# The down projection of a SwiGLU block: from a plain blocked product to Strassen's seven products

## The chip, the cores and the metric

The kernel runs on one core of a Trainium2 chip. Its engines work side by side, each on its own queue of instructions in a fixed order: PE (TensorE) multiplies matrices into PSUM, DVE (VectorE), ACT (ScalarE) and POOL (GpSimd) work elementwise, and SP (SyncE) issues loads and stores, which 16 DMA engines carry out. The metric is the device time of one execution in microseconds (us), lower being better.

## What is computed

One layer of an audio encoder on 1024 frames of width 1024, all in float32. The change touches only the last matrix product, `w_down`; the lines around it:

```python
x = x + rms_norm(mix, post_mix_g[l])
h2 = rms_norm(x, pre_ffn_g[l])
f = (jax.nn.silu(h2 @ w_gate[l]) * (h2 @ w_up[l])) @ w_down[l]
x = x + rms_norm(f, post_ffn_g[l])
```

`w_gate` and `w_up` are 1024 x 2816, `w_down` is 2816 x 1024. Below, f is the hidden activation, the product of silu(gate) and up; it is stored transposed, 22 blocks of 128 hidden rows by 1024 frames.

## The kernel before

**Precision.** Each float32 operand is split into a high half `hi` (ACT, L78, a cast) and a low half `lo` (DVE, L79, operand minus `hi`). A product then takes three matmuls: hi with hi, hi with lo, lo with hi (L103 to L105, or L1032 to L1034 in gate and up). Every matmul here is 128 x 128 stationary by 128 x 512 moving.

**Gate and up** (class `Gemm`, about 640 to 1098 us) already use Strassen's scheme in Winograd's form: 22 small products, a gate and an up product for each of 11 pairs p of hidden blocks, each made of seven sub-products q of 12 matmuls. POOL makes sums of weight pieces (`wsum`, L997), ACT and DVE split them into `whi` and `wlo` (four buffers each), PE multiplies into the PSUM banks `px`, `pz`, `py`, and ACT and DVE combine the results into `c` tiles. The sub-products of neighbouring gemms are interleaved by the list `order`. `finish` (L1058 to L1066) multiplies each up tile by its gate tile on DVE (L1065), and POOL stores it to `fd` in DRAM (L1066); four tiles of 128 x 512 belong to a pair p: two hidden blocks by two halves of the frames.

**Down** (`down_block`, `down_mm`, from L1092). The two column halves `dh` of the output are done one after the other. For each, eight PSUM banks hold the eight row tiles of the output, and PE runs over all 22 hidden blocks k: 8 row tiles x 3 matmuls for one k, so 2 x 22 x 8 x 3 = 1056 matmuls. The blocks k are fed in groups of mostly four: SP loads f (two tiles for a k, L1110) and `w_down` (one, L1114) into eight `raw` buffers (`wraw`, `ld`, `Td`), f is split into `fb`, of which there are two (tag `T`), and the weight into `whi` and `wlo`. Between the column halves the eight banks are read out: DVE copies (L1169), ACT sums squares (L1171), POOL multiplies by the gain (L1172). The last group of the second half runs row tile by row tile, with norm and store (L1126, L1127) right behind each.

**Order.** A scheduler fixes the order on every engine when the program is built. Loads and splits of a group stand under `tc.high_priority()`, so they come as early in the queues as free buffers allow; on ACT and DVE they can stand ahead of work that was written earlier. PSUM has eight banks: four of tag `b` (`pB`), two of `a` (`pA`), `c0` and `c1` (`pS`).

Of the kernel before, what the change touches and what calls it, by code (L numbers as in the profile page):

```python
# [41 lines left out]
def tile_hymba_trunk(ctx, tc, x, w_in, vecs, w_l, w2, a2, g2, w_o, w_gate, w_up, w_down,  # L42
# [21 lines left out]
    def v1(col):  # L64
# [1031 lines left out]
    def bank(i):
        if i < 4:
            return pB.tile([128, H], F32, name="pd", tag="b")
        if i < 6:
            return pA.tile([128, H], F32, name="pd", tag="a")  # L1100
        return pS.tile([128, H], F32, name="pd", tag=f"c{i - 6}")

    def down_block(ks, dh):
        fb = tp.tile([128, 4, 2, 2, H], F32R, name="fb", tag="T")
        ws = []
        with tc.high_priority():
            for n, k in enumerate(ks):
                for h in range(2):
                    raw = raw_tile([128, H])
                    sy.dma_start(out=raw, in_=fd[k][:, h * H:(h + 1) * H])  # L1110
                    split(raw, fb[:, n, h, 0], fb[:, n, h, 1])
                    if h == 0:
                        raw = raw_tile([128, H])
                        sy.dma_start(out=raw, in_=w_down[k * 128:(k + 1) * 128, dh * H:(dh + 1) * H])  # L1114
                        ws.append(wsplit(raw, [128, H]))
        return fb, ws

    def down_mm(ps, fb, ws, n, k, i):
        f = fb[:, n, i // 4]
        ts = slice((i % 4) * 128, (i % 4 + 1) * 128)  # L1120
        mm3(ps, f[:, 0, ts], f[:, 1, ts], ws[n][0], ws[n][1], k == 0, k == NHID - 1)

    def close(i, xts, rs):
# [5 lines left out]
    acc1 = {}  # L1129
    for dh, sizes in ((0, (4, 4, 4, 4, 4, 2)), (1, (4, 4, 4, 4, 2, 4))):  # L1130
        pd = [None] * 8
        k0 = 0
        for bn, size in enumerate(sizes):
            ks = range(k0, k0 + size)
            k0 += size
            fb, ws = down_block(ks, dh)
            if dh == 0 or bn < len(sizes) - 1:
                for n, k in enumerate(ks):
                    for i in range(8):
                        if k == 0:  # L1140
                            pd[i] = bank(i)
                        down_mm(pd[i], fb, ws, n, k, i)
                continue
            prev = None
            for i in range(8):
                xts = []
                for q in range(2):
                    xt = wt("xt", XT[(2 * i + q) % len(XT)], [128, H])
                    sy.dma_start(out=xt, in_=x1d[i * 128:(i + 1) * 128, q * H:(q + 1) * H])
                    xts.append(xt)  # L1150
                for n, k in enumerate(ks):
                    down_mm(pd[i], fb, ws, n, k, i)
                junk = wt("junk", "Vtok", [128, H])
                sc.activation(junk, pd[i], AF.Square, accum_out=ssqs[i][:, 1:2])
                a = acc1[i] = wt("acc1", "am", [128, H])
                ve.tensor_tensor(out=a, in0=pd[i], in1=gain[1][:, H:D], op=ALU.mult)
                ss = sp.tile([128, 1], F32, name="ss1", tag="ss1")
                gp.tensor_tensor(out=ss, in0=ssqs[i][:, 0:1], in1=ssqs[i][:, 1:2], op=ALU.add)
                rs = rsqrt_rows(sp, ss, D, "fo", gp)
                if prev:  # L1160
                    close(*prev)
                prev = (i, xts, rs)
            close(*prev)
        if dh == 0:
            for i in range(8):
                ssq = sp.tile([128, 2], F32, name="ssf", tag=f"ssf{i}", bufs=1)
                ssqs.append(ssq)
                a = wt("acc0", ("e", "ez")[i // 4], [128, H])
                ve.tensor_copy(out=a, in_=pd[i])  # L1169
                junk = wt("junk", "Vtok", [128, H])  # L1170
                sc.activation(junk, pd[i], AF.Square, accum_out=ssq[:, 0:1])  # L1171
# [68 lines left out]
```

## Time and profile before

| | us |
|---|---|
| time, median of 3 runs (1356.93 to 1358.76) | 1358.42 |
| the profiled execution's own time | 1353.48 |
| span from its first to its last instruction | 1351.7 |
| PE busy / DVE busy / ACT busy / POOL busy | 1287.8 / 882.7 / 505.3 / 332.6 |
| down projection, first to last matmul | 1086.4 to 1343.7 |

The profile is one execution. A row of an engine gives start and duration; "idle before" or the bracket behind a row is the time the engine stood still ahead of it and what ended that. Matmuls overlap, so their start-to-start distance, not their duration, is what one costs.

### The profile page before, as it was taken

How to read it: one execution, taken by the hardware profiler on the slowest of the kernel's cores; microseconds unless marked ns; L12 is line 12 of the kernel's file. 1: busy time of each engine (PE TensorE's matmuls, PEld its weight loads, DVE VectorE, ACT ScalarE, POOL GpSimd, SP SyncE). 2: the span in 40 equal slices, each digit the busy share in tenths (PEclk: the TensorE clock that was granted, in tenths of full speed). 3: DMA queues.
4: the chain of work that ended last, by engine and by line, in shares of the span. 5: the costliest groups of instructions: out<-in, count | busy, mean ns of one | idle time of the engine just before them, and what ended most of it. 6: DMA issues, size and time to landing. Idle time of an engine off the chain costs nothing.

```text
span 1351.7 us, 21475 instructions
## 1 busy us (share of the span) xinstructions
PE 1287.8 (95%) x8184; PEld 1027.6 (76%) x8184; DVE 882.7 (65%) x1690; ACT 505.3 (37%) x939; POOL 332.6 (25%) x376
## 2 busy tenths in 40 slices
PE   7999899999989999999889999999999989998997
PEld 5878767777767777677668888888888868887886
DVE  5999899988898885554885555455545453335335
ACT  7237336334322223434443333333333343234231
POOL 1122315232323111042533333323323200003002
PEclk9999899899989999999999999999999999999999
DMA  6116334222221103542312222222222274433525
GB/s 235 32 47 210 102 110 131 71 89 87 73 86 56 64 6 111 183 163 94 125 55 92 80 86 78 94 77 88 71 79 86 86 241 134 148 130 124 166 94 202
DMA packets 70663, 144.84 MB, mean 107 GB/s; under 512 B 8352, under 2 KB 8736, under 8 KB 70560
## 3 DMA queue, kind: packets, MB, share of 16 engines
q1 hardware_dynamic: 61376, 118.30, 27.1%
q0 software_dynamic: 5728, 18.88, 3.7%
q10 hardware_dynamic: 3456, 6.29, 1.2%
q8 instruction: 64, 1.05, 0.3%
q14 instruction: 39, 0.32, 0.1%
HBM read 106.74 MB, written 36.70 MB: 106 GB/s over the span
## 4 chain that ended last, share of the span: by engine, by line
PE 45%; DVE 2%; DMA 2%; issue 1%; ACT 1%; POOL 0%; DVEq 0%; SPq 0%; ACTq 0%; POOLq 0%
PE px L1032 5%; PE px L1033 5%; PE px L1034 5%; PE pd L104 5%; PE pd L103 5%; PE pd L105 5%; PE pz L1032 3%; PE pz L1033 3%; PE pz L1034 3%; PE py L1034 1%; PE py L1033 1%; PE py L1032 1%; DMA wraw<-fd 1%; DVE fb L79 1%; DVE wlo L79 0%
## 5 line engine op out<-in xcount | busy, mean ns | idle before, releaser
L79 DVE TENSOR_TENSOR wlo<-wraw,whi 128x512 fp32r<-128x512 f32 x155 | 109.5, 707 | 153.8 <-ACT whi L78 151.7
L78 ACT CAST whi<-wraw 128x512 fp32r<-128x512 f32 x155 | 95.9, 620 | 225.0 <-PE pd L105 77.5
L103 PE MATMUL pd<-whi,fb 128*128 128x512 f32 x352 | 137.4, 392 | 8.2 <-ACT junk L1171 4.0
L104 PE MATMUL pd<-wlo,fb 128*128 128x512 f32 x352 | 137.7, 391 | 0.0
L105 PE MATMUL pd<-whi,fb 128*128 128x512 f32 x352 | 137.6, 391 | 0.0
L79 DVE TENSOR_TENSOR fb<-wraw,fb 128x512 fp32r<-128x512 f32 x88 | 61.3, 737 | 70.4 <-ACT fb L78 70.0
L78 ACT CAST whi<-wsum 128x512 fp32r<-128x512 f32 x88 | 54.5, 619 | 122.5 <-PE py L1033 36.1
L79 DVE TENSOR_TENSOR wlo<-wsum,whi 128x512 fp32r<-128x512 f32 x88 | 66.8, 759 | 45.5 <-ACT whi L78 44.5
L250 DVE SCALAR_TENSOR_TENSOR cfa<-cfu,vec,cfa 128x512 f32<-128x512 f32 x120 | 92.4, 798 | 0.8
L997 POOL TENSOR_TENSOR wsum<-wraw 128x512 f32<-128x512 f32 x44 | 59.6, 1354 | 114.3 <-DMA wraw<-in_w_gate 42.2
L103 PE MATMUL prkv<-hT,whi 128*128 128x512 f32 x192 | 82.7, 430 | 2.6 <-DVE lz L369 2.6
L103 PEld LDWEIGHTS pd<-whi,fb 128*128 128x128 f32 x352 | 66.4, 189 | 24.0 <-ACT junk L1171 4.9
L575 DVE TENSOR_TENSOR tm<-TT,Mg 128x2 f32<-128x2 f32 (+30 forms) x248 | 79.4, 320 | 5.9
L78 ACT CAST fb<-wraw 128x512 fp32r<-128x512 f32 x88 | 50.5, 619 | 77.0 <-PE pd L105 43.4
L105 PE MATMUL prkv<-hT,wlo 128*128 128x512 f32 x192 | 78.8, 410 | 0.0
L104 PE MATMUL prkv<-hT,whi 128*128 128x512 f32 x192 | 78.4, 408 | 0.0
L105 PEld LDWEIGHTS pd<-whi,fb 128*128 128x128 f32 x352 | 66.5, 189 | 14.1
L104 PEld LDWEIGHTS pd<-wlo,fb 128*128 128x128 f32 x352 | 66.5, 189 | 13.6
L1032 PE MATMUL px<-h2T,whi 128*128 128x512 f32 x176 | 70.1, 398 | 1.8 <-ACT c L1046 1.4
L1033 PE MATMUL px<-h2T,whi 128*128 128x512 f32 x176 | 69.5, 395 | 0.0
L1034 PE MATMUL px<-h2T,wlo 128*128 128x512 f32 x176 | 69.4, 394 | 0.0
L577 DVE TENSOR_REDUCE TT<-tm 128x1 f32<-128x2 f32 (+30 forms) x248 | 62.9, 253 | 5.8
(335 smaller groups left out, 3155.5 us busy)
## 6 DMA issues: line engine op xcount, KB each, us to landing
wraw<-fd SPq DMA_DIRECT2D x88, 256.0 KB, 3.6
wraw<-in_w_in SPq DMA_DIRECT2D x44, 256.0 KB, 2.9
wraw<-in_w_gate SPq DMA_DIRECT2D x44, 256.0 KB, 2.8
wraw<-in_w_up SPq DMA_DIRECT2D x44, 256.0 KB, 2.8
fd<-c POOLq DMA_DIRECT2D x44, 256.0 KB, 2.3
wraw<-in_w_down SPq DMA_DIRECT2D x44, 256.0 KB, 3.3
xt<-in_x SPq DMA_DIRECT2D x16, 512.0 KB, 4.6
mix<-m POOLq DMA_DIRECT2D x24, 256.0 KB, 2.4
```

The costliest lines, as they stand in the source:

```text
L78: sc.copy(hi, raw)
L79: ve.tensor_tensor(out=lo, in0=raw, in1=hi.bitcast(F32), op=ALU.subtract)
L103: te.matmul(ps, lhsT=lhi, rhs=rhi, start=start, stop=False)
L104: te.matmul(ps, lhsT=lhi, rhs=rlo, start=False, stop=False)
L105: te.matmul(ps, lhsT=llo, rhs=rhi, start=False, stop=stop)
L250: ve.scalar_tensor_tensor(out=acc, in0=u[:, q:q + H], scalar=v1(V_CFW + i * 31 + q), in1=acc, op0=ALU.mult, op1=ALU.add)
L575: ve.tensor_tensor(out=tm[:, 0:ni, 0:t + 1], in0=TT[:, 0:ni, 0:t + 1], in1=Mg[:, t, 0:t + 1].unsqueeze(1).to_broadcast([128, ni, t + 1]), ...
L577: ve.tensor_reduce(out=TT[:, 0:ni, t:t + 1], in_=tm[:, 0:ni, 0:t + 1], axis=AX.X, op=ALU.add)
L997: gp.tensor_tensor(out=t, in0=x, in1=y, op=op)
L1032: te.matmul(ps, lhsT=hi[:, k, :], rhs=rhi, start=first and k == 0, stop=False, skip_group_check=True)
L1033: te.matmul(ps, lhsT=hi[:, k, :], rhs=rlo, start=False, stop=False, skip_group_check=True)
L1034: te.matmul(ps, lhsT=lo[:, k, :], rhs=rhi, start=False, stop=k == 3, skip_group_check=True)
```

## The change

The down projection is done by the same seven-product scheme. The output is seen as 2 x 2 blocks (two halves of the frames by two column halves), f and `w_down` as 2 x 2 blocks for each pair p of hidden blocks (first or second block of the pair). A step is one product q of one pair p: its f operand (128 x 512) and its weight operand (128 x 512) are each split in two, and it takes 4 row tiles x 3 = 12 matmuls. There are 7 x 11 = 77 steps, so 924 matmuls, in the order of `PQ`: all pairs of product 1, then of 5, 6, 3, 7, 2, 4. The products 1, 6, 7, 4 accumulate in the four banks `X` (tag `b`), 5, 3, 2 in `Z` (tags `a`, `c0`, `c1`); behind each product `after` reads its banks out while the next product uses the other four.

The f operands that are sums (products 5, 6, 7, 3) are made under gate and up: `finish` makes four sums `fs` on DVE for each pair, and POOL stores them by one DMA of 1 MB to `fsd`; of the four f tiles three are still stored. The weight operands that are sums are made on DVE in the down projection (`d_operand`), 44 subtractions in all. Both operands of a step go through `ob` (tag `T`, two buffers of four steps each); the weights no longer go through `whi` and `wlo`. The groups are 18 of four steps, one of one, one of four, and the last runs row tile by row tile.

The core of the diff:

```diff
-    t2r = mp.tile([128, 4, H], F32, name="t2r")
+    t2r = wt("t2r", "t2r", [128, 4, H])
...
-                gp.dma_start(out=fd[2 * self.p + b][:, h * H:(h + 1) * H], in_=dst)
+                f = self.done
+                f[b, h] = dst
+                q = {(0, 0): 1, (1, 0): 2, (1, 1): 4}.get((b, h))
+                if q:
+                    gp.dma_start(out=fd[q, self.p], in_=dst)
+                if len(f) == 4:
+                    fs = wt("fs", "t2r", [128, 4, H])
+                    for n, (x, y, op) in enumerate(((f[0, 1], f[1, 1], ALU.add), (fs[:, 0], f[0, 0], ALU.subtract),
+                                                    (f[0, 0], f[0, 1], ALU.subtract), (f[1, 0], fs[:, 1], ALU.subtract))):
+                        ve.tensor_tensor(out=fs[:, n], in0=x, in1=y, op=op)
+                    gp.dma_start(out=fsd[self.p], in_=fs)
...
+    PQ = [1, 5, 6, 3, 7, 2, 4]
+    steps = [(q, p) for q in PQ for p in range(NP)]
...
+        if q == 5:
+            if p % 2 == 0:
+                t = wt("tres", ("AR", "ZA")[p // 2 % 2], [128, 2, H])
+                tres[p], tres[p + 1] = t[:, 0], t[:, 1]
+            x, y = d_raw(p, 0, 1), d_raw(p, 0, 0)
+            ve.tensor_tensor(out=tres[p], in0=x, in1=y, op=ALU.subtract)
+            return tres[p]
+        if q == 6:
+            x = d_raw(p, 1, 1)
+            ve.tensor_tensor(out=tres[p], in0=x, in1=tres[p], op=ALU.subtract)
+            return tres[p]
+        x = d_raw(p, 0 if q == 7 else 1, 0)
+        a, b = (tres[p], x) if q == 7 else (x, tres[p])
+        ve.tensor_tensor(out=x, in0=a, in1=b, op=ALU.subtract)
+        return x
...
+    def down_block(block):
+        ob = tp.tile([128, 4, 2, 2, H], F32R, name="ob", tag="T")
         with tc.high_priority():
+            for n, (q, p) in enumerate(block):
+                split(f_raw(q, p), ob[:, n, 0, 0], ob[:, n, 0, 1])
+                split(d_operand(q, p), ob[:, n, 1, 0], ob[:, n, 1, 1])
+        return ob
+
+    def down_mm(q, p, ob, n, t):
+        f, w = ob[:, n, 0], ob[:, n, 1]
+        ts = slice(t * 128, (t + 1) * 128)
+        ps = (Z if q in (5, 3, 2) else X)[t]
+        st, en = q in (1, 5, 2) and p == 0, p == NP - 1
+        te.matmul(ps, lhsT=f[:, 0, ts], rhs=w[:, 0], start=st, stop=False, skip_group_check=True)
+        te.matmul(ps, lhsT=f[:, 0, ts], rhs=w[:, 1], start=False, stop=False, skip_group_check=True)
+        te.matmul(ps, lhsT=f[:, 1, ts], rhs=w[:, 0], start=False, stop=en, skip_group_check=True)
...
+    KEPT = {1: ["e"] * 4, 5: ["ez"] * 4, 6: ["am"] * 3 + ["hs"]}
...
+    def after(q, t):
+        if q in KEPT:
+            k = kept[q, t] = wt("kept", KEPT[q][t], [128, H])
+            sc.copy(k, (Z if q == 5 else X)[t])
+        elif q == 3:
+            c = kept[6, t]
+            ve.tensor_tensor(out=c, in0=Z[t], in1=c, op=ALU.add)
+            square(t, 1, c)
+            scaled(c, 1, gp)
...
+        else:
+            square(4 + t, 0, X[t])
+            a = wt("c21", "bv", [128, H])
+            ve.tensor_tensor(out=a, in0=X[t], in1=gain[1][:, 0:H], op=ALU.mult)
+            row_out(4 + t, (a, kept[5, t]), *row_scale(4 + t))
+
+    sizes = [4] * 18 + [1, 4]
```

Three places show how the built order moves. First DVE in gate and up, behind the last tile of a pair (`c` with two numbers is the multiplication by the gate tile; `wlo` is a low half of a gate or up weight). Before:

```order
L1065 TENSOR_TENSOR c_9781<-c_9781,c_9629 128x512
L79 TENSOR_TENSOR wlo<-wraw,whi 128x512 x2
L79 TENSOR_TENSOR wlo<-wsum,whi 128x512
L1050 TENSOR_TENSOR c_9972<-pz,c_9972 128x512
L1062 TENSOR_TENSOR c_9972<-c_9972,sig 128x512
```

After:

```order
L1066 TENSOR_TENSOR c_9843<-c_9843,c_9691 128x512
L1076 TENSOR_TENSOR fs<-c_9843,c_9884 128x512
L1076 TENSOR_TENSOR fs<-c_9712,c_9843 128x512
L79 TENSOR_TENSOR wlo<-wraw,whi 128x512
L1076 TENSOR_TENSOR fs<-fs,c_9712 128x512
L1076 TENSOR_TENSOR fs<-c_9928,fs 128x512
L79 TENSOR_TENSOR wlo<-wraw,whi 128x512
L79 TENSOR_TENSOR wlo<-wsum,whi 128x512
```

Two of the four sums now stand ahead of each of the next two low halves; the rest of the round is as it was, in ten of the eleven pairs.

Second PE where the last gemm's products 7 and 4 (`px<-h2T`) meet the first matmuls of down. Before (`fb` is f, `pd` a bank):

```order
L1034 MATMUL px<-yT,wlo 128x512
L103 MATMUL pd<-whi,fb 128x512 x5
L1032 MATMUL px<-h2T_7228,whi 128x512
```

After (`pdx` is a bank of `X`, L1156 to L1158 the three matmuls of `down_mm`):

```order
L1035 MATMUL px<-yT,wlo 128x512
L1156 MATMUL pdx<-ob 128x512
L1157 MATMUL pdx<-ob 128x512
L1158 MATMUL pdx<-ob 128x512
L1156 MATMUL pdx<-ob 128x512
L1157 MATMUL pdx<-ob 128x512
L1158 MATMUL pdx<-ob 128x512
L1156 MATMUL pdx<-ob 128x512
L1157 MATMUL pdx<-ob 128x512
L1158 MATMUL pdx<-ob 128x512
L1156 MATMUL pdx<-ob 128x512
L1033 MATMUL px<-h2T_7250,whi 128x512
```

Ten matmuls of down instead of five now stand ahead of the gemm's product 7.

Third DVE inside the down projection: four groups of low halves before, and a group of product 5 after (`tres` is a weight sum, `ob<-wraw` an f, `ob<-tres` a weight). Before:

```order
L79 TENSOR_TENSOR fb<-wraw,fb 128x512 x4
L79 TENSOR_TENSOR wlo<-wraw,whi 128x512
L79 TENSOR_TENSOR fb<-wraw,fb 128x512 x2
L79 TENSOR_TENSOR wlo<-wraw,whi 128x512
L79 TENSOR_TENSOR fb<-wraw,fb 128x512 x2
L79 TENSOR_TENSOR wlo<-wraw,whi 128x512 x2
```

After:

```order
L1132 TENSOR_TENSOR tres<-wraw 128x512 x3
L79 TENSOR_TENSOR ob<-wraw,ob 128x512
L79 TENSOR_TENSOR ob<-tres,ob 128x512
L79 TENSOR_TENSOR ob<-wraw,ob 128x512
L79 TENSOR_TENSOR ob<-tres,ob 128x512
L79 TENSOR_TENSOR ob<-wraw,ob 128x512
L79 TENSOR_TENSOR ob<-tres,ob 128x512
L79 TENSOR_TENSOR ob<-wraw,ob 128x512
```

The weight subtractions stand ahead of the group's low halves, since their loads need no room in `ob`.

## Rows read from the trace of the kernel before

**Rows 1.** The page, part 1: busy us, share of the span, instructions.

```profile
span 1351.7 us, 21475 instructions
...
PE 1287.8 (95%) x8184; PEld 1027.6 (76%) x8184; DVE 882.7 (65%) x1690; ACT 505.3 (37%) x939; POOL 332.6 (25%) x376
```

**Rows 2.** Windows: length, busy us per engine, granted clock, DMA share, GB/s.

```profile
700.00:1060.00 360.00, 359.67 (x1567) 293.98 (x1566) 190.11 (x264) 131.24 (x227) 119.97 (x113) 1.00 0.24 83
...
1104.00:1344.00 240.00, 235.95 (x1032) 194.41 (x1030) 95.81 (x142) 73.85 (x143) 18.97 (x30) 0.99 0.44 140
```

**Rows 3.** Groups by line from 800 us on: busy, mean ns, idle before.

```profile
L104 PE MATMUL pd<-wlo,fb 128*128 128x512 f32 x352 | 137.7, 391 | 0.0
...
L79 DVE TENSOR_TENSOR fb<-wraw,fb 128x512 fp32r<-128x512 f32 x88 | 61.3, 737 | 70.4 <-ACT fb L78 70.0
L79 DVE TENSOR_TENSOR wlo<-wraw,whi 128x512 fp32r<-128x512 f32 x87 | 60.0, 690 | 129.3 <-ACT whi L78 127.3 <-DMA wraw<-fd 2.0
...
L1065 DVE TENSOR_TENSOR c<-c,c 128x512 f32<-128x512 f32 x24 | 20.7, 864 | 0.2
...
L1065 DVE TENSOR_TENSOR c<-px,c 128x512 f32<-128x512 f32 x8 | 5.5, 691 | 9.1 <-PE px L1034 9.1
```

**Rows 4.** Timeline of PE: first and last of 55 matmuls running.

```profile
1209.63 0.39 PE L105 MATMUL pd<-whi,fb 128*128 128x512 f32 x1
...
1221.88 0.39 PE L105 MATMUL pd<-whi,fb 128*128 128x512 f32 x1
```

**Rows 5.** Timeline of PE halfway, where the second column half begins.

```profile
1228.88 0.80 PE L103 MATMUL pd<-whi,fb 128*128 128x512 f32 x1 [3.98 <-ACT junk L1171]
1229.47 0.63 PE L104 MATMUL pd<-wlo,fb 128*128 128x512 f32 x1
...
1232.39 0.40 PE L103 MATMUL pd<-whi,fb 128*128 128x512 f32 x1
```

**Rows 6.** Windows right behind that wait.

```profile
1228.80:1232.10 3.30, 3.22 (x8) 2.57 (x9) 1.98 (x3) 1.67 (x4) 0.60 (x1) 0.51 0.48 151
```

**Rows 7.** Timeline of PE at the start of the down projection.

```profile
1084.48 0.39 PE L1034 MATMUL px<-yT,wlo 128*128 128x512 f32 x1
1086.41 1.45 PE L103 MATMUL pd<-whi,fb 128*128 128x512 f32 x5 [1.54 <-ACT whi L78]
1087.70 0.46 PE L1032 MATMUL px<-h2T,whi 128*128 128x512 f32 x1
...
1098.94 0.50 PE L103 MATMUL pd<-whi,fb 128*128 128x512 f32 x1 [1.13 <-DVE c L1065]
...
1102.08 0.51 PE L103 MATMUL pd<-whi,fb 128*128 128x512 f32 x1 [1.48 <-DVE c L1055]
```

**Rows 8.** Timeline: four low halves on DVE (start, us taken).

```profile
1080.56 2.49 DVE L79 TENSOR_TENSOR fb<-wraw,fb 128x512 fp32r<-128x512 f32 x4
```

**Rows 9.** Timeline of ACT: a block of high halves, from its release on.

```profile
1120.30 2.18 ACT L78 CAST fb<-wraw 128x512 fp32r<-128x512 f32 x4 [4.82 <-PE pd L105]
...
1126.41 0.62 ACT L78 CAST fb<-wraw 128x512 fp32r<-128x512 f32 x1 [1.47 <-DMA wraw<-fd]
```

**Rows 10.** The page, part 6: KB of one load, us from issue to landing.

```profile
wraw<-fd SPq DMA_DIRECT2D x88, 256.0 KB, 3.6
```

**Rows 11.** Window at that start: the densest loads.

```profile
1090.00:1100.00 10.00, 8.87 (x39) 6.69 (x38) 6.80 (x11) 4.09 (x8) 1.64 (x3) 1.00 0.91 302
```

**Rows 12.** Timeline of ACT in gate and up: one high half.

```profile
1021.31 0.62 ACT L78 CAST whi<-wsum 128x512 fp32r<-128x512 f32 x1 [2.14 <-PE py L1033]
```

**Rows 13.** Timeline of POOL in gate and up: after a store.

```profile
1027.30 0.56 POOL L1066 DMA_DIRECT2D fd<-c  x1
1031.33 1.29 POOL L997 TENSOR_TENSOR wsum<-wraw 128x512 f32<-128x512 f32 x1 [3.47 <-DMA wraw<-in_w_gate]
```

**Rows 14.** Timeline of the end.

```profile
1343.71 0.39 PE L105 MATMUL pd<-whi,fb 128*128 128x512 f32 x1
...
1347.04 1.41 DVE L1126 SCALAR_TENSOR_TENSOR acc<-acc,for,xt 128x512 f32<-128x512 f32 x2 [0.57 <-DMA xt<-x1d]
```

More of the change, by code (lines that the diff above doesn't have):

```diff
@@ L1092, in tile_hymba_trunk @@
     load_gain(1, "KB")
-    acc0, ssqs = [], []
     XT = ["AK"] * 2 + ["Lo"] * 2 + ["Atok"] * 2
[L1096 to L1105, printed above, removed]
-        with tc.high_priority():
[L1107 to L1123, printed above, removed]
-        for dh in range(2):
-            a = (acc0[i], acc1[i])[dh]
+    PQ = [1, 5, 6, 3, 7, 2, 4]
+    steps = [(q, p) for q in PQ for p in range(NP)]
+    tres = {}
+    def f_raw(q, p):
+        raw = raw_tile([128, H])
+        sy.dma_start(out=raw, in_=fd[q, p] if q in (1, 2, 4) else fsd[p][:, {5: 0, 6: 1, 7: 2, 3: 3}[q]])
+        return raw
@@ new lines, in d_raw, with d_operand @@
+    def d_raw(p, j, dh):
+        raw = raw_tile([128, H])
+        r0 = (2 * p + j) * 128
+        sy.dma_start(out=raw, in_=w_down[r0:r0 + 128, dh * H:(dh + 1) * H])
+        return raw
+    def d_operand(q, p):
+        if q == 1:
+            return d_raw(p, 0, 0)
+        if q == 2:
+            return d_raw(p, 1, 0)
+        if q == 3:
+            return d_raw(p, 1, 1)
+        if q == 5:
[13 more added lines that the diff above has]
+        return x
@@ new lines, in tile_hymba_trunk, with square, scaled, row_scale @@
+    X, Z = [], []
+    kept = {}
+    KEPT = {1: ["e"] * 4, 5: ["ez"] * 4, 6: ["am"] * 3 + ["hs"]}
+    ssq = {}
+    def square(i, dh, src):
+        if i not in ssq:
+            ssq[i] = sp.tile([128, 2], F32, name="ssf", tag=f"ssf{i}", bufs=1)
+        junk = wt("junk", "Vtok", [128, H])
+        sc.activation(junk, src, AF.Square, accum_out=ssq[i][:, dh:dh + 1])
+    def scaled(a, dh, eng):
+        eng.tensor_tensor(out=a, in0=a, in1=gain[1][:, dh * H:(dh + 1) * H], op=ALU.mult)
+    def row_scale(i):
+        xts = []
+        for dh in range(2):
+            xt = wt("xt", XT[(2 * i + dh) % len(XT)], [128, H])
+            sy.dma_start(out=xt, in_=x1d[i * 128:(i + 1) * 128, dh * H:(dh + 1) * H])
+            xts.append(xt)
+        ss = sp.tile([128, 1], F32, name="ss1", tag="ss1")
+        gp.tensor_tensor(out=ss, in0=ssq[i][:, 0:1], in1=ssq[i][:, 1:2], op=ALU.add)
+        return xts, rsqrt_rows(sp, ss, D, "fo", gp)
@@ L1126, in close, with row_out @@
+    def row_out(i, cs, xts, rs):
+        for dh in range(2):
+            a = cs[dh]
             ve.scalar_tensor_tensor(out=a, in0=a, scalar=rs, in1=xts[dh], op0=ALU.mult, op1=ALU.add)
             sy.dma_start(out=out[i * 128:(i + 1) * 128, dh * H:(dh + 1) * H], in_=a)
[L1129 to L1171, printed above, removed]
-                gp.tensor_tensor(out=a, in0=a, in1=gain[1][:, 0:H], op=ALU.mult)
-                acc0.append(a)
@@ new lines, in after @@
+    def after(q, t):
[7 more added lines that the diff above has]
+            scaled(c, 1, gp)
+        elif q == 7:
+            c = kept[5, t]
+            ve.tensor_tensor(out=c, in0=X[t], in1=c, op=ALU.add)
+            square(4 + t, 1, c)
+            scaled(c, 1, gp)
+        elif q == 2:
+            c = kept[1, t]
+            ve.tensor_tensor(out=c, in0=Z[t], in1=c, op=ALU.add)
+            square(t, 0, c)
+            scaled(c, 0, gp)
+            row_out(t, (c, kept[6, t]), *row_scale(t))
+        else:
[3 more added lines that the diff above has]
+            row_out(4 + t, (a, kept[5, t]), *row_scale(4 + t))
@@ new lines, in tile_hymba_trunk @@
+    sizes = [4] * 18 + [1, 4]
+    s0 = 0
+    for bn, size in enumerate(sizes):
+        block = steps[s0:s0 + size]
+        s0 += size
+        ob = down_block(block)
+        if bn == len(sizes) - 1:
+            for t in range(4):
+                for n, (q, p) in enumerate(block):
+                    down_mm(q, p, ob, n, t)
+                after(q, t)
+            continue
+        for n, (q, p) in enumerate(block):
+            if p == 0 and q == 1:
+                X += [pB.tile([128, H], F32, name="pdx", tag="b") for t in range(4)]
+            elif p == 0 and q == 5:
+                Z += [pA.tile([128, H], F32, name="pdz", tag="a") for t in range(2)]
+                Z += [pS.tile([128, H], F32, name="pdz", tag=f"c{t}") for t in range(2)]
+            for t in range(4):
+                down_mm(q, p, ob, n, t)
+            if p == NP - 1:
+                for t in range(4):
+                    after(q, t)
```

5 lines of the change are left out of this document (3 added, 2 removed).

## The prediction

> **What bounds the kernel now.** I read the page's first part, then windows over the two stages that the change touches, then PE's timeline for what one matmul costs and for each wait in the down projection. PE is busy for 95% of the span and no other engine for more than 65% [rows 1]. By stage it is sharper: in gate and up, from 700 to 1060 us, PE stands still for 0.33 of 360 us while DVE is busy for 190; in the down projection, from 1104 to 1344 us, PE works 236 of 240 us, with DVE at 96, ACT at 74 and the DMA engines at 0.44 [rows 2]. So in both stages the other engines wait for PE, and time is won only by giving PE less to do or by taking away one of its few waits. The group row of a down matmul says 391 ns [rows 3], but that is a duration, and durations overlap: between the starts of the first and the last of 55 matmuls in a row lie 12.25 us, 12.25 / 54 = 0.2269 us for each [rows 4]. The sum goes by 0.2269; by 391 ns the gain would come out 1.7 times too large.
>
> **The change, part by part.**
>
> *Matmuls.* Before there are 2 x 22 x 8 x 3 = 1056, after 77 x 12 = 924 of the same shape. 132 x 0.2269 = 29.9 us less PE work. This is the main term; it holds in full only if PE stays fed.
>
> *The change of column half goes.* Halfway PE waited 3.98 us until the eight banks had been read, and then ran slowly: eight matmul distances from 1228.88 to 1232.39 took 3.51 us where 8 x 0.2269 = 1.82 are due [rows 5], with a granted clock of 0.51, its lower level of 1.2 GHz [rows 6]. Together 3.98 + 1.69 = 5.7 us. After the change each product reads out four banks while the next product works on the other four for 132 x 0.2269 = 29.9 us; the readout is four ACT copies or four DVE sums, under 1 us each. So all 5.7 us go. If the readout came late, the cover would have to shrink from 29.9 to some 4 us first.
>
> *The start.* PE waits there for 1.54, 1.13 and 1.48 us [rows 7], 4.2 in all. The third is for a `pz` bank, and product 1 uses only banks of tag `b`: it goes. At the first, PE waited for the third load of the group, split; now the first two loads are enough, and ten matmuls (2.3 us) instead of five lie ahead of the gemm's product 7, which could start only at 1087.70 because ACT copied the bank late. I take a gain of 2.5 us. The ends: all 4.2 gained, or 4 lost, since fifteen low halves of `ob` stand on DVE ahead of the last gemm's readouts, and seven of these belong to the second group and wait for loads. PE's next multiplication into that gemm's `pz` bank would then wait for them.
>
> *Feeding PE in down.* A step lasts 12 x 0.2269 = 2.72 us. Four low halves in a row take DVE 2.49 us, 0.62 each [rows 8]. A step of product 5 needs three such operations, 1.87 us, of products 1, 3 and 2 two; four high halves take ACT 2.18 us [rows 9], so a step 1.1 us. Both fit into 2.72 us. Loads: product 5 takes three of 256 KB a step (0.786 MB in 2.72 us is 289 GB/s), for 11 steps; 6, 7, 4 and the rest two (193 GB/s). The eight buffers must turn over in 8 / 3 x 2.72 = 7.25 us in product 5. A turn is 3.6 us from issue to landing [rows 10], then 0.62 and 0.69 us for the split, 4.9 us, and 2.3 us are left. The densest 10 us of before moved 302 GB/s with the DMA engines at 0.91 [rows 11], so 289 is near what can be had but below it. What hides a late load is the second `ob` buffer: a group is split while the one before it is multiplied for 4 x 2.72 = 10.9 us, and its DVE work is 4 x 1.87 = 7.5 us. In the before kernel a group's ACT work, with its waits for loads, ran from 1120.30 to past 1126.41 [rows 9], for twelve splits instead of eight. I take 0. The ends: 0, and +8 us if a turn takes 10 us (then a product-5 step takes 10 x 3 / 8 = 3.75 us, 11 x 1.03 = 11 us more, of which at most one group's slack of 3.4 us is hidden).
>
> *Four sums a pair in gate and up.* 44 DVE operations at about 0.7 us, 31 us, go into a stage in which DVE idles for 47%. Two stand ahead of each of two low halves, so a low half comes at most 1.4 us later. Its cover: ACT makes the high half as soon as PE has read the buffer for the last time [rows 12], and with four buffers three products of 2.72 us lie between; less the two halves of the split, 8.2 - 1.3 = 6.9 us. POOL's 1 MB store now waits for the fourth sum, some 3.4 us later than the store of before, and the weight sums are queued behind it; there POOL idled 3.47 us until a load came [rows 13], and the sums run ahead over five buffers. I take 0. The ends: 0, and 44 x 0.62 = 27 us if every sum came on PE's path.
>
> *The same SBUF ports for DVE and POOL.* Multiplications with both inputs in SBUF take 864 ns on average, with one in PSUM 691 [rows 3]: 0.17 us more, 0.7 for four sums, which the 6.9 us cover. The Trainium skill (SBUF — State Buffer, Who interferes with whom) says that a DVE instruction with two SBUF inputs and a GpSimd instruction that reads SBUF block each other for a whole instruction. The row agrees that something is lost, but on average far less than a whole instruction; what full blocking would cost is the third rival.
>
> *The end.* The last group may enter its buffer only when the group of four before the single step is through, so 2.72 us of cover are left for eight splits. The eighth low half is ready after about 0.6 + 8 x 0.62 = 5.6 us, and PE asks for it 2.72 + 3 x 0.68 + 0.23 = 5.0 us after. A loss of 0.6 us; ends 0 and 3 (a load late). Behind the last matmul the chain stays as it is: from 1343.71 over ACT, POOL and the last DVE operations at 1347.04 to the stores [rows 14].
>
> *Sum.* 29.9 + 5.7 + 2.5 - 0.6 = 37.5 us. The profiled execution took 1353.48 us, 1.8 more than its span, so one like it would take 1316.0. The median of the three timed runs is 4.9 us above it; the same difference from that gives 1320.9. I predict **1321 us**.
>
> **The rivals.**
>
> *The loads of products 5 to 4 are late* (+8 us, 1329). For it: 289 of 302 GB/s, and f loads hold their buffers until `ob` is free. Against it: the second group buffer, and only 11 of 77 steps are that dense. It decides when a buffer's turn exceeds 7.25 us.
>
> *The start loses instead of gaining* (4 - (-2.5) = 6.5 us, 1327.5). It decides if DVE's readout of the last gemm's `pz` comes more than 8.6 us after product 6 ends: ten matmuls, product 7, four matmuls and product 4 are 38 x 0.2269 us.
>
> *DVE and POOL block each other in gate and up.* With each sum held for a POOL sum of 1.29 us [rows 13], four take 4 x 1.98 = 7.9 us and a low half between them 0.7, 8.6 against a cover of 6.9: 1.7 us for each of ten pairs, 17 us, 1338. Against it is the mean of 864 ns. By the Trainium skill's rule named above, this is the case.
>
> *Slower than before.* In gate and up, one ring: the fourth sum waits behind a low half that itself waits for a buffer from PE, the store on POOL for the fourth sum, the next gemm's weight sums for the store, and PE for these. If a turn takes longer than the cover, PE waits in every pair. The kernel turns slower from 37.5 / 10 = 3.75 us a pair on, a turn of 6.9 + 3.75 = 10.7 us; at 6 us a pair it would be 1381. Against it: five sum buffers ahead, and PE's 0.33 us of idleness now.
>
> **How the numbers follow.** The forecast has 0.63, loads 0.17, the start 0.09, blocking 0.06, slower 0.05. The low end is all of the start gained and no loss at the end, 1318.6, less the 4.9 us by which single executions differ: 1314. The high end takes loads and start together, 1321 + 8 + 6.5 = 1335.5, and so leaves out blocking and the slower case. 0.2% of this kernel, 2.7 us, is about what a measurement can tell from no change. Faster: all but the slower case and a little for the unseen, 0.93; within 0.2% 0.02; slower 0.05.
>
> **What would show it.** Right: PE's down groups with 924 matmuls at the same distance, no wait of 4 us with a low clock in the middle, PE idle under 1 us from 700 to 1060 us in spite of a DVE busy share some 9 points higher, and down about 220 us long. Wrong: PE waiting for `ob` splits that wait for DMA in product 5, some 30 to 60 us into down; `wlo` late after every second round; or a wait for `pz` at the start.

## The result, and the profile after

The changed kernel takes **1317.09 us** (median of 4 runs, 1316.52 to 1322.24) where the kernel before takes 1357.68 (4 runs beside them, 1356.24 to 1358.76). The ratio is 0.971, with a 95% interval of 0.9684 to 0.9737: 36 to 43 us less by that interval. The prediction was 1321 us, 1314 to 1336. The profiled execution took 1317.35 us, with a span of 1315.6 instead of 1351.7 us. Executions of one kernel differ by 14 us and more: six of the changed kernel on one chip took 1313.77 to 1327.84 us, and the longest of these, which was profiled, began its down projection 12.5 us later than the execution below and was no slower within it.

The first part of the page, against [rows 1]:

```profile
PE 1256.0 (95%) x8052; PEld 1001.6 (76%) x8052; DVE 953.0 (72%) x1800; ACT 519.7 (40%) x973; POOL 339.4 (26%) x380
```

PE did 31.8 us less work and still fills 95% of a shorter span. DVE rose from 882.7 to 953.0 us, and still idles for 28%. Windows over the stages, against [rows 2]; the third lies over loads of product 5, which run ahead of its matmuls (1124.07 to 1153.76), the fourth behind the first row tile of the last group:

```profile
700.00:1060.00 360.00, 359.67 (x1567) 294.00 (x1566) 217.99 (x301) 130.99 (x227) 119.74 (x113) 1.00 0.30 103
1104.00:1310.00 206.00, 201.85 (x882) 166.01 (x880) 138.94 (x212) 91.54 (x182) 26.71 (x35) 0.99 0.65 213
1114.00:1144.00 30.00, 30.00 (x134) 24.84 (x133) 16.56 (x26) 13.73 (x26) 0.00 (x0) 1.00 0.84 269
1292.00:1300.00 8.00, 5.20 (x15) 3.53 (x14) 6.76 (x11) 2.46 (x5) 0.94 (x1) 0.79 0.73 245
```

Gate and up carry 27.9 us more of DVE work (217.99 against 190.11), and PE's 359.67 us have not moved. In the third window, the densest in loads, PE runs without a gap at 269 GB/s. The one place where PE stands still for long is the last window. PE's timeline, from the last matmul ahead of the down projection to its own last one; the answers to [rows 5] and [rows 7] are in it:

```profile
1084.01 0.39 PE L1035 MATMUL px<-yT,wlo 128*128 128x512 f32 x1
1084.24 0.39 PE L1156 MATMUL pdx<-ob 128*128 128x512 f32 x1
...
1087.91 0.50 PE L1033 MATMUL px<-h2T,whi 128*128 128x512 f32 x1 [1.24 <-ACT c L1047]
...
1153.76 0.39 PE L1158 MATMUL pdz<-ob 128*128 128x512 f32 x1
1153.99 0.39 PE L1156 MATMUL pdx<-ob 128*128 128x512 f32 x1
...
1273.67 0.39 PE L1156 MATMUL pdx<-ob 128*128 128x512 f32 x1
...
1292.71 0.39 PE L1156 MATMUL pdx<-ob 128*128 128x512 f32 x1
1295.65 0.50 PE L1157 MATMUL pdx<-ob 128*128 128x512 f32 x1 [2.56 <-DVE ob L79]
...
1296.86 0.79 PE L1157 MATMUL pdx<-ob 128*128 128x512 f32 x1 [0.24 <-DVE ob L79]
...
1308.26 0.39 PE L1158 MATMUL pdx<-ob 128*128 128x512 f32 x1
```

From product 5 to product 6 (1153.76 to 1153.99) the distance is the usual 0.23 us: the readouts between products cost PE nothing (the other changes of product are in a table below). Product 4 is another matter. From 1273.67 to 1308.26, and 0.23 for the last matmul, it takes 34.8 us for 132 matmuls that are due in 29.95: **4.9 us are lost there**, 2.8 in the two waits and the rest at the slower clock behind them (0.79 in the fourth window above).

What DVE and POOL did ahead of that wait, from their timelines and ACT's, in order of time (L1187 is a row output, L111 the last step of its scale, L1172 the gain):

```profile
1287.09 1.30 POOL L1172 TENSOR_TENSOR kept<-kept,gain 128x512 f32<-128x512 f32 x1 [4.09 <-ACT junk L1169]
...
1289.49 1.78 DVE L1187 SCALAR_TENSOR_TENSOR kept<-kept,for,xt 128x512 f32<-128x512 f32 x1 [2.63 <-POOL for L111]
...
1290.19 4.27 ACT L78 CAST ob<-wraw 128x512 fp32r<-128x512 f32 x8 [2.52 <-PE pdx L1158]
...
1292.98 1.42 DVE L1187 SCALAR_TENSOR_TENSOR kept<-kept,for,xt 128x512 f32<-128x512 f32 x2 [0.45 <-POOL for L111]
1294.31 4.90 DVE L79 TENSOR_TENSOR ob<-wraw,ob 128x512 fp32r<-128x512 f32 x8
```

ACT began the last group's high halves at 1290.19, but DVE began their low halves only at 1294.31. In between it was kept by the row outputs of product 2, which wait for POOL. That the row outputs, and not the short cover, are the cause is so far only read from one trace; three runs below test it.

### The profile page after: what moved, and what is told of

Same layout as the page of the kernel before. It is cut to its first block, busy times and chain, and to the rows that moved or that the text cites. A ratio compares the mean times of both kernels' runs of the same rounds, so it can differ in the third digit from the quotient of the medians.

```text
span 1315.6 us, 21385 instructions
## 1 busy us (share of the span) xinstructions
PE 1256.0 (95%) x8052; PEld 1001.6 (76%) x8052; DVE 953.0 (72%) x1800; ACT 519.7 (40%) x973; POOL 339.4 (26%) x380
## 4 chain that ended last, share of the span: by engine, by line
PE 46%; DVE 2%; POOL 1%; issue 1%; ACT 0%; DMA 0%; DVEq 0%; POOLq 0%; ACTq 0%
PE px L1033 6%; PE px L1034 6%; PE px L1035 6%; PE pz L1033 3%; PE pz L1034 3%; PE pz L1035 3%; PE pdx L1157 3%; PE pdx L1158 3%; PE pdx L1156 2%; PE pdz L1157 2%; PE pdz L1156 2%; PE pdz L1158 2%; PE py L1035 1%; PE py L1033 1%; PE py L1034 1%; DVE ob L79 1%
## 5 line engine op out<-in xcount | busy, mean ns | idle before, releaser
L78 ACT CAST whi<-wraw 128x512 fp32r<-128x512 f32 x111 | 68.6, 620 | 145.9 <-PE px L1034 57.9
L79 DVE TENSOR_TENSOR wlo<-wraw,whi 128x512 fp32r<-128x512 f32 x111 | 81.0, 732 | 51.0 <-ACT whi L78 50.8
L79 DVE TENSOR_TENSOR ob<-wraw,ob 128x512 fp32r<-128x512 f32 x132 | 86.1, 706 | 28.3 <-ACT ob L78 28.0
L78 ACT CAST ob<-wraw 128x512 fp32r<-128x512 f32 x132 | 73.3, 619 | 77.7 <-PE pdx L1158 39.3
L79 DVE TENSOR_TENSOR wlo<-wsum,whi 128x512 fp32r<-128x512 f32 x88 | 69.5, 790 | 45.0 <-ACT whi L78 44.5
L1157 PE MATMUL pdx<-ob 128*128 128x512 f32 x176 | 69.3, 394 | 2.8 <-DVE ob L79 2.8
L1156 PE MATMUL pdx<-ob 128*128 128x512 f32 x176 | 69.0, 393 | 0.0
L1158 PE MATMUL pdx<-ob 128*128 128x512 f32 x176 | 68.8, 392 | 0.0
L676 ACT ACTIVATE S<-pny,Pc 128x64 f32<-128x64 f32 x64 | 20.2, 315 | 100.9 <-PE pny L673 100.8
L1172 POOL TENSOR_TENSOR kept<-kept,gain 128x512 f32<-128x512 f32 x12 | 16.8, 1414 | 166.7 <-ACT junk L1169 166.7
L1156 PE MATMUL pdz<-ob 128*128 128x512 f32 x132 | 51.3, 389 | 0.0
```

Of the source, the lines that this page charges most:

```text
L78: sc.copy(hi, raw)
L79: ve.tensor_tensor(out=lo, in0=raw, in1=hi.bitcast(F32), op=ALU.subtract)
L1156: te.matmul(ps, lhsT=f[:, 0, ts], rhs=w[:, 0], start=st, stop=False, skip_group_check=True)
L1157: te.matmul(ps, lhsT=f[:, 0, ts], rhs=w[:, 1], start=False, stop=False, skip_group_check=True)
L1158: te.matmul(ps, lhsT=f[:, 1, ts], rhs=w[:, 0], start=False, stop=en, skip_group_check=True)
```

## The experiments

The time of a run is the median of its timed executions; where few microseconds matter, the profiled executions are compared stage by stage.

**Is PE's work really what is saved?** The 132 matmuls are put back, with no other work:

```diff
+        if q == 7:
+            te.matmul(Z[t], lhsT=f[:, 0, ts], rhs=w[:, 0], start=p == 0, stop=False, skip_group_check=True)
+            te.matmul(Z[t], lhsT=f[:, 0, ts], rhs=w[:, 1], start=False, stop=False, skip_group_check=True)
+            te.matmul(Z[t], lhsT=f[:, 1, ts], rhs=w[:, 0], start=False, stop=en, skip_group_check=True)
```

> The changed kernel, with 132 matmuls put back: in each of the eleven steps of product 7, 12 extra matmuls of the same operands go into the four banks that are idle then. No load, split or sum is added. If PE alone sets the pace of the down projection, the whole of 132 x 0.2269 = 29.9 us comes back: 1317.1 + 29.9 = 1347 us, and product 7 takes 60 instead of 30 us. The rival: PE is paced by its feed (loads, or splits on DVE and ACT), and the extra matmuls fill time in which it would wait later. Then clearly less than 25 us comes back, under 1342 us.

1347.11 us, 30.0 more than the changed kernel (29.0 without the longest of its ten runs, 1360.63); the span grew by 28.7, to 1344.3. Product 7 took 59.84 us, from 1213.22 to 1273.06, instead of 29.92. A window over it:

```profile
1213.00:1272.00 59.00, 59.00 (x262) 48.86 (x261) 23.60 (x35) 16.85 (x36) 7.98 (x6) 1.00 0.33 107
```

PE ran through all of it, while the DMA share fell to 0.33. So the main term is shown: in this product PE alone sets the pace, and a matmul that is not made is worth its 0.227 us.

**The halfway wait, in the kernel before.** Only the place of the readout in the queues is changed:

```diff
-                ve.tensor_copy(out=a, in_=pd[i])
-                junk = wt("junk", "Vtok", [128, H])
-                sc.activation(junk, pd[i], AF.Square, accum_out=ssq[:, 0:1])
+                with tc.high_priority():
+                    ve.tensor_copy(out=a, in_=pd[i])
+                    junk = wt("junk", "Vtok", [128, H])
+                    sc.activation(junk, pd[i], AF.Square, accum_out=ssq[:, 0:1])
```

> The kernel before, with nothing changed but the place in the queues of the readout between the column halves: the eight DVE copies and ACT squares stand under high priority, so that the copies come ahead of the five high-priority low halves that stood in front of them. The theory: the halfway wait of 3.98 us and the slow clock of 1.69 us behind it were a matter of that queue, and 5.7 us of the change's gain could have been had without it: ratio to the kernel before 0.9958, PE without a wait over 1 us halfway. The rival: PE waits there because eight banks have to be read by one engine before it may go on, whatever the order: then the first banks come earlier, but a wait of 2 us or more remains and the gain is under 3 us.

1350.1 against 1355.36 us, 5.3 less, ratio 0.9946 (0.9919 to 0.9974). DVE's timeline halfway, a window over the same stretch, and PE's longest wait at the start, with ACT's wait for a load ahead of it:

```profile
1216.15 4.87 DVE L1170 COPY acc<-pd 128x512 f32<-128x512 f32 x8
...
1200.00:1240.00 40.00, 40.00 (x178) 33.15 (x177) 24.34 (x31) 17.70 (x39) 11.86 (x8) 1.00 0.46 152
...
1102.09 0.80 PE L103 MATMUL pd<-whi,fb 128*128 128x512 f32 x1 [5.53 <-DVE c L1055]
...
1097.15 0.62 ACT L78 CAST fb<-wraw 128x512 fp32r<-128x512 f32 x1 [4.53 <-DMA wraw<-fd]
```

The wait is gone, PE is busy for all 40 us of the window: eight copies in 4.87 us free a bank every 0.61 us, and PE asks for one every 3 x 0.227 = 0.68. In the kernel before, seven of the copies ran from 1214.95 us on, and the eighth stood behind five low halves:

```profile
1219.35 7.50 DVE L79 TENSOR_TENSOR fb<-wraw,fb 128x512 fp32r<-128x512 f32 x5
...
1227.37 0.68 DVE L1169 COPY acc<-pd 128x512 f32<-128x512 f32 x1
```

So this term was a matter of the queue, and could have been had without the other scheme. The start shows something else: the wait that took 1.48 us in [rows 7] took 5.53 here, with DVE's order there unchanged, because a load came late (ACT waited 4.53 us for it). That stall is not a constant of the kernel.

**Four sums a pair, twice and four times.** The edit is a factor 2 (or 4) ahead of the list of sums in `finish`:

```diff
-                    for n, (x, y, op) in enumerate(((f[0, 1], f[1, 1], ALU.add), (fs[:, 0], f[0, 0], ALU.subtract),
+                    for n, (x, y, op) in 2 * list(enumerate(((f[0, 1], f[1, 1], ALU.add), (fs[:, 0], f[0, 0], ALU.subtract),
...
```

> The changed kernel with each of the four f sums of a pair made twice on DVE under gate and up (the same values, so 44 sums and some 30 us of DVE more); the store of a pair waits for the last of them. If the sums are covered by the 6.9 us between PE's last use of a weight buffer and its next, and a low half then comes up to 2.8 us late, nothing changes: within 2 us of the changed kernel, PE idle under 1 us from 700 to 1060 us. If DVE and POOL block each other for whole instructions (the rival of the prediction), low halves come 16 us late at every pair and PE waits: 17 us or more.

> The same with each sum made four times: 132 sums and some 90 us of DVE more. Up to eight of them stand ahead of each of two low halves, which then come 5.5 us late, near the 6.9 us of cover, and DVE would be busy for about 309 of 360 us. By the cover: 0 to 10 us more (up to 1 us a pair), PE waiting for low halves at some pairs. If the cover is really that of all buffers ahead and not 6.9 us: within 2 us of the changed kernel. If sums cost PE time directly (blocking): 40 us and more.

1318.1 and 1320.23 us, spans 1315.8 and 1317.1. The windows from 700 to 1060 us, twofold, then fourfold:

```profile
700.00:1060.00 360.00, 359.67 (x1567) 293.96 (x1566) 254.51 (x338) 130.45 (x226) 125.44 (x113) 1.00 0.30 103
```

```profile
700.00:1060.00 360.00, 358.76 (x1560) 292.16 (x1559) 312.99 (x407) 128.34 (x224) 172.46 (x113) 1.00 0.30 102
```

At twice the sums PE lost nothing, at four times 0.9 us in the window, with DVE at 87%. So the change's own sums were far from PE's path: by the estimate above, low halves may come some 5 us late before PE feels it. Whether the cover is 6.9 us or more, the fourfold run does not tell, since its 0.9 us lies where both expectations meet. A blocking that costs PE 17 us and more is ruled out; whether DVE and POOL block each other at all, PE's time does not tell (rows on that stand further down).

**Fewer buffers, and more loads.** First four load buffers instead of eight, then one more load of 256 KB a step that nothing reads:

```diff
+    RAWS[:] = ["ld"] * 4
+    rawn[0] = 0
```

```diff
+        sy.dma_start(out=raw_tile([128, H]), in_=w_down[2 * p * 128:(2 * p + 1) * 128, 0:H])
```

> The changed kernel with four load buffers in the down projection instead of eight; everything else is unchanged. The theory (the turn of a buffer sets the pace of the feed): at a turn of 4.9 to 5.4 us, product 5, with three loads a step, gets a step in 5.2 x 3 / 4 = 3.9 us instead of 2.72, 11 x 1.2 = 13 us less the slack of one group, about +10 us, and PE waits for splits within product 5; the products with two loads a step need 2.6 us and stay just covered. The rival: the turn under this load is longer (8 us or so), then all products slow down, a step of two loads takes 4 us and the whole costs 60 us or more; or loads are served so fast (turn under 3.6 us) that nothing changes.

> The changed kernel with one more load of 256 KB in each step of the down projection, into a buffer that nothing reads: product 5 would need four loads a step, 1.05 MB in 2.72 us or 385 GB/s, the other products three, 289 GB/s. If 302 GB/s is about what can be had, product 5 takes 1.05 MB / 302 GB/s = 3.47 us a step, 11 x 0.75 = 8.2 us more, less up to 3 us of slack: +5 to +8 us, PE waiting in product 5 alone, and the others are unharmed. If the load path is what nearly bounds the whole projection, products 6 to 4 wait as well, +15 us or more. If nothing changes, far more than 302 GB/s can be had.

Four buffers: 1342.62 us; the profiled execution took 1337.63, with a span 20.3 longer than the changed kernel's. More loads: 1359.33 us, span 42.0 longer. By product, from the first matmul of one to that of the next (29.92 us where PE never waits):

| product | 5 | 6 | 3 | 7 | 2 | 4 |
|---|---|---|---|---|---|---|
| changed kernel | 29.92 | 29.92 | 29.92 | 29.92 | 29.92 | 34.82 |
| four buffers | 33.74 | 31.42 | 29.92 | 32.43 | 31.65 | 45.46 |
| one more load a step | 41.88 | 36.64 | 29.92 | 32.47 | 32.30 | 50.40 |

With four buffers, product 5's step is 33.74 / 11 = 3.07 us, so a buffer turns over in about 3.07 x 4 / 3 = 4.1 us. That is less than the 4.9 to 5.4 expected, so product 5 lost 3.8 us and not 10; it is far under the 7.25 us from which the eight buffers would have been short. The DMA view of its product 5 says why (issues, KB each, median us to landing):

```profile
wraw<-in_w_down SPq DMA_DIRECT2D x18, 256.0 KB, 3.0
wraw<-fs SPq DMA_DIRECT2D x10, 256.0 KB, 3.3
```

With fewer loads on their way, each landed in 3.0 to 3.3 us, against about 4 in the changed kernel. The run with more loads went beyond its first expectation, 5 to 8 us in product 5 alone: 12.0 us were lost there, and products 6, 7 and 2 lost 6.7, 2.6 and 2.4, as the second had it. Its windows over product 5, and over the products that followed:

```profile
1124.00:1166.00 42.00, 34.80 (x134) 26.39 (x133) 23.36 (x37) 16.98 (x30) 0.00 (x0) 0.92 0.83 267
1174.00:1232.00 58.00, 57.99 (x248) 47.47 (x247) 31.79 (x50) 25.85 (x45) 0.00 (x0) 0.97 0.84 274
```

44 loads of 0.262 MB in 41.88 us are 275 GB/s, so over tens of microseconds some 270 is what this feed of eight buffers reached, not the 302 of the ten densest in [rows 11]; as the DMA engines' share was 0.83, it is not shown that they could do no more. The changed kernel's product 5 wants 289: its 8.65 MB need 32.0 us at 270 GB/s where 29.9 are there. Its trace shows what gave way. The weight's low half of product 5's first step was ready 12.1 us before PE asked for it, that of its tenth step only 1.5 us, 1148.78 less 1147.30, and in product 6 the least was 1.8:

```profile
1146.61 0.69 DVE L79 TENSOR_TENSOR ob<-tres,ob 128x512 fp32r<-128x512 f32 x1
...
1148.78 0.39 PE L1157 MATMUL pdz<-ob 128*128 128x512 f32 x1
```

So the term was right, with 1.5 us to spare.

Neither theory expected what both runs lost in product 4, 11 and 16 us more than the changed kernel. In the run with more loads PE waited there for 6.09, 4.12 and 2.89 us. Rows of DVE and PE for the first of these, and of the queue that issues loads and of DVE for the last:

```profile
1317.73 1.74 DVE L1188 SCALAR_TENSOR_TENSOR kept<-kept,for,xt 128x512 f32<-128x512 f32 x1 [0.72 <-POOL for L111]
1319.39 1.28 DVE L79 TENSOR_TENSOR ob<-wraw,ob 128x512 fp32r<-128x512 f32 x2
...
1320.73 0.79 PE L1158 MATMUL pdx<-ob 128*128 128x512 f32 x1 [6.09 <-DVE ob L79]
...
1330.46 0.38 SPq L1118 DMA_DIRECT2D wraw<-in_w_down  x1
...
1337.40 0.69 DVE L1141 TENSOR_TENSOR wraw<-wraw,tres 128x512 f32<-128x512 f32 x1 [4.67 <-DMA wraw<-in_w_down]
```

The first wait is for low halves that stood on DVE behind row outputs, 5 us after their high halves were made; ahead of the second's low halves DVE waited 2.71 us for POOL at a row output. This is the cause that the next runs test in the changed kernel. The third is for a load that was issued only at 1330.46: stores of product 2's rows, which wait for DVE, stood ahead of it in the queue. In the changed kernel the queue waited 11.9 us for row outputs between 1264 and 1300 us, with enough loaded ahead.

**The last group: a longer cover, or no row outputs.** The first kernel gives the last group three steps of cover, the second leaves out the row outputs of product 2:

```diff
-    sizes = [4] * 18 + [1, 4]
+    sizes = [4] * 17 + [2, 3, 4]
```

```diff
-            row_out(t, (c, kept[6, t]), *row_scale(t))
+            for dh, a in ((0, c), (1, kept[6, t])):
+                sy.dma_start(out=out[t * 128:(t + 1) * 128, dh * H:(dh + 1) * H], in_=a)
```

> The changed kernel with its last groups cut otherwise: 17 groups of four steps, then two, three and four, instead of 18 of four, then one and four. The last group's splits then have three steps, 8.2 us, ahead of them instead of one, 2.7 us. The theory (the cover is short): the 2.80 us of waiting at the last group and the slow clock behind it, 4.8 us in all, go, 1312.3 us, ratio to the changed kernel 0.9964. The rival: DVE is held by the row outputs of product 2, which wait for POOL, and these are where they were: the wait remains wholly or for the most part, less than 2 us is gained.

> The changed kernel with the row outputs of product 2 left out: for the first four row tiles the scale and the residual sum are not made, and the two unscaled halves are stored as they are; the squares and the gain are still made, groups and loads are unchanged. The theory (row outputs on DVE that wait for POOL delay the low halves of the last group): the wait at the last group shrinks to 0.6 us or less and the slow clock behind it goes, so the loss of 4.8 us falls to about 1, 1313 us. The rival (the cover of one step is too short by itself): 2 us or more of the wait remain, 1316 us or more.

More cover: 1315.12 us, span 1315.5; product 4 took 34.76 us, as before. The wait went for the most part to the group of three ahead of the last, whose low halves (six, from 1285.97 on) now stood behind row outputs that wait for POOL, as the timelines of PE and DVE show:

```profile
1287.31 0.50 PE L1157 MATMUL pdx<-ob 128*128 128x512 f32 x1 [2.03 <-DVE ob L79]
...
1297.58 0.50 PE L1156 MATMUL pdx<-ob 128*128 128x512 f32 x1 [0.69 <-ACT ob L78]
...
1284.04 1.42 DVE L1187 SCALAR_TENSOR_TENSOR kept<-kept,for,xt 128x512 f32<-128x512 f32 x2 [0.72 <-POOL for L111]
...
1285.97 3.69 DVE L79 TENSOR_TENSOR ob<-wraw,ob 128x512 fp32r<-128x512 f32 x6
```

Without the row outputs: 1318.69 us by the clock of four runs (1313.95 to 1321.39, too far apart for 4 us), but in the profile the span is 1312.2 and the whole loss is gone:

```profile
1275.25 0.39 PE L1156 MATMUL pdx<-ob 128*128 128x512 f32 x1
...
1305.21 0.39 PE L1158 MATMUL pdx<-ob 128*128 128x512 f32 x1
...
1292.42 4.91 DVE L79 TENSOR_TENSOR ob<-wraw,ob 128x512 fp32r<-128x512 f32 x8 [0.76 <-ACT ob L78]
```

Product 4 takes 30.19 us, and DVE now waits for ACT ahead of the low halves. The cover theory falls, and the row outputs remain as the cause. Leaving them out also takes away their scales and loads, so the next kernel keeps all the work.

**The same work without the wait for POOL.** Two more kernels, with the changed kernel beside them as their base. In the first the gain of product 2 goes to DVE, and the row outputs behind all four sums; the second also leaves high priority off the second group.

```diff
-    ssq = {}
+    ssq, scales = {}, {}
...
-            scaled(c, 0, gp)
-            row_out(t, (c, kept[6, t]), *row_scale(t))
+            scaled(c, 0, ve)
+            scales[t] = row_scale(t)
+            if t == 3:
+                for i in range(4):
+                    row_out(i, (kept[1, i], kept[6, i]), *scales[i])
```

```diff
-        with tc.high_priority():
+        with tc.high_priority() if block[0] != (1, 4) else nullcontext():
```

> The changed kernel itself once more, on the chip of the next two, as their base: 1317 us, ratio to the kernel before 0.971; the wait of about 2.6 us for a low half in the last group and the slow clock behind it, 4.8 us together, and 1.2 us of waiting at the start.

> The changed kernel with everything computed, but in the readout of product 2 the gain is multiplied on DVE instead of POOL, and the row outputs of the four row tiles are written after all four sums, gains and scales instead of tile by tile. POOL's part for a row falls from about 2.5 to 1.2 us, and on DVE the sums no longer stand behind row outputs that wait for POOL. If those waits are what made the last group late, the wait and the slow clock go as in the run with the row outputs left out: profiled span 1315.6 - 4 = 1311.6 us, ratio to the changed kernel 0.997. The rival (DVE has too much work there, whoever it waits for): DVE gets four more operations and the wait stays at 2 us or more, no gain.

> The kernel of the run just above, and besides the second group of the down projection (product 1, pairs 4 to 7) is split without high priority, so that on ACT three and on DVE seven of its splits no longer stand ahead of the last gate and up readouts. The theory: the start wait of 1.2 to 2.8 us for ACT's copy (L1047) goes, some 1.2 us less than the run above in the profile. The rival: the second group is then late itself, and PE waits for it instead, as long or longer.

Medians of 6 runs each: the changed kernel 1316.81 us, the first 1312.40, the second 1312.91. Against the kernel before they stand at 0.9693 (0.9652 to 0.9735), 0.9645 (0.961 to 0.968) and 0.965 (0.9613 to 0.9687). PE's and DVE's timelines of the first:

```profile
1275.85 0.39 PE L1156 MATMUL pdx<-ob 128*128 128x512 f32 x1
...
1305.81 0.39 PE L1158 MATMUL pdx<-ob 128*128 128x512 f32 x1
...
1289.31 3.40 DVE L1187 SCALAR_TENSOR_TENSOR kept<-kept,for,xt 128x512 f32<-128x512 f32 x5
1293.02 4.91 DVE L79 TENSOR_TENSOR ob<-wraw,ob 128x512 fp32r<-128x512 f32 x8 [0.32 <-ACT ob L78]
```

Product 4 is back at 30.19 us although DVE has four operations more. The 4.4 us between the medians fit the 4.6 us of that product, but the two intervals overlap a little; what the profile shows is that the wait is gone, and with it that the waits for POOL are the cause. Which of the two edits did it, the gain's engine or the place of the row outputs, was not tried apart. The span is 1313.2 us where 1311.6 were expected, since this execution came to the down projection 2.2 us later (1086.42 against 1084.24). The second kernel's start wait is 0.72 us, for the next copy of ACT's (L1050), where the first's is 1.21, for L1047: half a microsecond less where 1.2 were expected, and nothing in the time. The first is the best of these kernels, 1312.4 us.

## Why the prediction was right, step by step

- **Matmuls, -29.9.** Right: the same distance of 0.227 us, and product 7 took 29.92 us longer with the 132 matmuls put back.
- **Halfway, -5.7.** Right: no wait between any two products, and 5.3 us were gained in the kernel before by the order of its queue alone. The term was a little small: from start to start, the matmuls of the kernel before lost 6.2 us there.
- **The start, -2.5.** Near: waits of 4.15 us [rows 7] became 1.24, 2.9 less, and from start to start, with the slower matmuls behind the waits, a loss of 5.5 us became 1.7. The three waits named are gone; the new one is for ACT's copy, which freed the bank of the gemm's product 7 no sooner than before. Over the runs that leave this place alone that wait went from 0.58 us to 2.59, so a part of the gain is luck.
- **Feed, 0.** Right in the sum. The turn was put at 4.9 us and is about 4.1 with four buffers; the rate was compared with 302 GB/s, and about 270 is what was reached over a product, so the reserve was smaller than the text makes it: 1.5 us at the tenth step.
- **Four sums, 0, and ports, 0.** Right in the sum, but not by the reason given for the ports. PE's idleness from 700 to 1060 us stayed 0.33 us, DVE rose by 7.7 points where some 9 were expected. The groups of that stretch give the price of a sum with both inputs in SBUF and of POOL's weight sum:

```profile
L998 POOL TENSOR_TENSOR wsum<-wraw 128x512 f32<-128x512 f32 x37 | 47.8, 1292 | 71.0 <-DVE wlo L79 25.8 <-DMA wraw<-in_w_up 16.6 <-ACT c L1041 13.2
...
L1076 DVE TENSOR_TENSOR fs<-c,c 128x512 f32<-128x512 f32 x18 | 14.6, 849 | 0.3
```

  A mean of 849 ns looks far from the 1.98 us of the blocking rival, as the 864 of [rows 3] did, and from this the prediction argued that far less than a whole instruction is lost. Single rows say otherwise. Of the 36 sums in that stretch 33 took 0.68 or 0.69 us and three 1.67; each of the three began while a POOL sum ran and ended 0.55 us behind it:

```profile
832.41 1.60 POOL L998 TENSOR_TENSOR wsum<-wraw,wsum 128x512 f32<-128x512 f32 x1 [5.43 <-issue]
...
832.90 1.67 DVE L1076 TENSOR_TENSOR fs<-c,c 128x512 f32<-128x512 f32 x1
```

  The same holds for all 41 TENSOR_TENSOR instructions of DVE with both inputs in SBUF that began during a POOL sum from 700 to 1060 us: each ended 0.5 to 0.6 us behind it, while the seven with an input in PSUM took 0.68 or 0.69 us as ever. The Trainium skill (SBUF — State Buffer, SBUF: two separate sides) says that of a DVE instruction with two SBUF inputs and a GpSimd instruction that reads SBUF the one that starts first has the shared ports for the whole instruction, and the other blocks; this trace agrees. What the rival had wrong is the number: 3 of 36 sums were held, not every one, and each for some 1.0 us, which the cover took. Nothing lost is right, by that cover and by how seldom the two met, not by the mean.
- **The end, +0.6.** This is the term that failed: 4.9 us. It counted the last group's eight splits against one step of cover, and left out what stood ahead of them on DVE, the row outputs of product 2 with their waits for POOL, and the slow clock behind a wait. Its upper end, 3, named a late load, which was not it either.
- **The sum.** 37.5 us were predicted between profiled executions, 1353.48 to 1316.0; measured were 36.1, to 1317.35. From start to start the matmuls give 29.95, halfway 6.2, the start 3.7 and the end -4.9, 35.0 us together; the stretch behind the last matmul is 0.7 shorter (8.0 against 7.3 us), and the last matmul ahead of down starts 0.5 sooner (1084.01 against 1084.48 in [rows 7]). So 1316.0 came near partly by luck: 4.3 us more were lost at the end than predicted, and 2.9 more were gained in four other places. That 1321 was 3.9 too high has another cause: 4.9 us were added by which the median of the kernel before lies above its profiled execution, and here the median lies 0.3 below it.
- **The rivals.** None came about. Loads were not late, the start gained, DVE and POOL blocked each other too seldom for PE to feel it, and the ring did not close even with four times the sums.

## What to carry to other kernels

Where one engine is busy for 95% of the span, work taken from it is worth its full start-to-start price, and what was added elsewhere costs nothing as long as it has a cover that can be named; that cover can be tested by multiplying the added work. At a last group, count on every engine what the queue holds ahead of its splits, above all work that waits for a third engine: a longer cover does not help against an instruction that stands in front and waits. A stall at a readout is first a question of the order of the queue, which can be tried by itself. And a mean duration is no evidence against a long wait that comes seldom: look at single rows.

## What was not expected of the hardware

When DVE was made busy for 313 of 360 us, it was POOL that paid: its weight sums rose from 1292 to 2481 ns on average, while DVE's sums stayed at 785 to 894 ns by group (POOL's group of the fourfold run):

```profile
L998 POOL TENSOR_TENSOR wsum<-wraw 128x512 f32<-128x512 f32 x37 | 91.8, 2481 | 127.9 <-DVE wlo L79 42.3 <-DMA wraw<-in_w_gate 31.2 <-issue 25.1
```

Here too the mean hides two kinds: seven of the 37 took 6.5 to 7.3 us, the others 1.3 to 1.8. During each of the seven DVE ran instructions with both inputs in SBUF, one right behind the other, until it came to one that reads PSUM (`pz`), and 1.23 or 1.24 us after that one's start, about what a sum takes on POOL alone, POOL's sum was over. One of the seven, with DVE's two rows:

```profile
838.65 7.06 POOL L998 TENSOR_TENSOR wsum<-wraw 128x512 f32<-128x512 f32 x1 [4.89 <-DVE wlo L79]
...
843.87 0.68 DVE L1076 TENSOR_TENSOR fs<-c,c 128x512 f32<-128x512 f32 x1
844.47 0.68 DVE L1051 TENSOR_TENSOR c<-pz,c 128x512 f32<-128x512 f32 x1
```

So a POOL sum that finds DVE at work on two SBUF inputs can stand still for ten DVE instructions in a row. That it is the ports that hold it is read from this pattern; no run was made for it.
